# A two-block network on one core: an overflow branch moved behind the tenth of eleven expert passes, a first gather in halves, 8 KB weight runs and 512-column products

## The chip, the cores and the metric

One core of a Trainium2 chip runs the whole program, with batch 1 and 256 tokens. The metric is the device time of one execution in microseconds (us); the kernel before takes 1347.06 us, the median of three runs.

## The reference

The network has two blocks of two layers each, on 256 tokens with D = 1024, in float32. The change touches the feed-forward networks of the first block and the mixtures of experts of the second:

```python
def conv_glu_ffn(n, w_up, conv_w, conv_b, w_down):          # D_FF = 2816
    gate, up = jnp.split(n @ w_up, 2, axis=-1)
    gp = jnp.pad(gate, ((0, 0), (CONV_WIDTH - 1, 0), (0, 0)))
    conv = conv_b
    for j in range(CONV_WIDTH):
        conv = conv + gp[:, j:j + s] * conv_w[j]
    return (jax.nn.silu(conv) * up) @ w_down

def hier_moe(h, w_group, b_group, w_expert, b_expert, w_gate, w_up, w_down):
    ...            # the best of 4 groups by softmax, the best 2 of its 8 experts
    for g in range(N_GROUPS):
        a = jnp.einsum('nd,edf->nef', t, w_gate[g])
        b = jnp.einsum('nd,edf->nef', t, w_up[g])
        hid = jax.nn.silu(a) * b * combine[:, g, :, None]
        y = y + jnp.einsum('nef,efd->nd', hid, w_down[g])

def hybrid_layer(x, ...):
    ...            # three mixers side by side, w_in before and w_out behind them
    x = x + jnp.einsum('bsm,md->bsd', mixed, w_out)
    x = x + hier_moe(rms_norm_2(x, norm2_g), ...)
```

## The kernel before

In the order of time the program is: a hybrid mixer, FFN 0, a differential mixer, FFN 1 (block 1), then mixer2(0), moe(0), mixer2(1), moe(1) and the final norm (block 2). Layers of block 2 are written l=0 and l=1.

**Products in float32.** TensorE (PE) takes operands of a rounded type at full rate, so a dense product is made of three: each operand is split into a high part (ACT copies it into the rounded type) and a low part (DVE subtracts that from the value), and `mm3` (L273 to L278) adds high x high, high x low and low x high into one PSUM accumulator. For weights the parts are called whi (L241) and wlo (L242).

**The FFN** (L656 to L725) goes over D_FF in 11 groups of 256 gate and 256 up columns. `up(g)` loads and splits the weights, and makes two accumulators of 128 x 2 x 256, pa for the gate and pb for up, tokens along the columns: for each of two halves f of the group's columns, for each of the two and each of 8 k-slices, one `mm3` with 256 columns. Then DVE multiplies the gate by the rows' norm (gt, L692), ACT and DVE make the convolution (L696, L699), ACT the silu (L701), POOL a product (L702), DVE the product with pb (L703), and hh and hl (L260, L261) are the parts of the result. `down(g)` makes 24 matmuls of 512 columns into four accumulators; PE does `up(g + 1)` before `down(g)`, and at the end `down(10)` comes straight behind `down(9)`.

**The experts.** Per layer 32 experts go through in 11 passes of 3 (the last has 2). A pass has 128 slots in four quarters of 32: one for each expert and one more for the fullest expert of the three, whose number PE loads into a register (`load_most`, TENSOR_LOAD of most). Each pass has three pieces of weights, each of 3 MB (2 MB in the last pass): the first half of gate and up over k, the second half, and down. 33 pieces go through six places of SBUF in turn. SP issues them, one after the other, in the order of the program; a piece is issued when PE has read the last of the piece that lay in its place. Gate and up pieces have runs of 4 KB in memory; a down piece is loaded by two DMAs in runs of 4 KB (L1291).

Before pass 0, `moe` makes the router's logits, the norm (`stats`), the parts nh and nl of the tokens (L1047, L1041) and from the logits each token's experts and slots: a row of small DVE instructions from lg (L1051) over mask (L1065) to the one-hot matrix oh (L1252). `gather` (L1256) multiplies tokens by oh on PE, 32 matmuls for two passes (L1266), and ACT and DVE take the columns out by turns (xg, L1268 and L1269). `expert_pass` (L1299) then does: the slots' weights (L1311 to L1320, ohT, cq, cw), 32 matmuls of gate and up with 512 columns (L1328; the profile counts each twice), hid (L1335, L1336), its transposes (L1239), 16 matmuls of down (L1347), the parts yh and yl (L260, L261), and the scatter back to tokens (L1355), which the schedule puts between the next pass's halves.

**The overflow branch.** If a token does not fit its expert's slots, a slow loop computes it; `most_tokens` reads the largest overflow, and each engine branches on it. In these inputs the loop is not taken. The branch stands behind pass 3 (j == 3), with the pieces up to 17 issued ahead of it. On SP, the skipped block (L1169) still waits for every DMA lane and counts it up, one event for each of eight lanes; other engines whose later instructions wait for a lane in the new count wait for that event.

**Between the layers.** When moe(0) frees places, SP loads the weights of mixer2(1) into them (L230; the first two loads, of 416 columns, are split by ACT and DVE in pieces of 128 x 832), and later the first six pieces of l=1.

Of the kernel before, what the change touches and what calls it, by code (L numbers as in the profile page):

```python
# [119 lines left out]
class Net:  # L120
# [196 lines left out]
    def prep_T(self, pool, g, bufs=2):  # L317

        nc = self.nc
        hi, lo = self.big(pool, bufs)  # L320
# [335 lines left out]
    def ffn(self, l):  # L656
# [4 lines left out]
        with self.pool("ffn", 2) as pl:  # L661
# [3 lines left out]
            nT = self.prep_T(pl, self.g("ffn_norm", l))  # L665
# [11 lines left out]
            def up(g):  # L677
# [13 lines left out]
                gt = pl.tile([P, 2, S], F32, name="gt")  # L691
                nc.vector.tensor_tensor(gt, pg, rB, OP.mult)  # L692
# [10 lines left out]
                nc.vector.tensor_tensor(c, c, pu, OP.mult)  # L703
# [25 lines left out]
    def mixer2(self, l):  # L729
        nc, a = self.nc, self.a  # L730
        w = a["w_in_2"][l]
        with self.pool("hring2", 2) as self.hp, self.pool("mixT") as pt, \
# [143 lines left out]
            self.pooling(pl, pw, u, gp, oT)  # L876
            self.out_proj(oT, None, 1)
# [121 lines left out]
    def load_router(self, l):  # L999
# [11 lines left out]
        nc.vector.tensor_tensor(wr, wr, self.g("norm2_g_2", l)[:, :, None].to_broadcast([P, KD, 36]), OP.mult)  # L1011
        self.router = wr, br, gp

    def moe(self, l):
        nc, tc, a = self.nc, self.tc, self.a
        with self.pool("xb", XB, side="right") as xb, self.pool("moeh") as ph, \
# [17 lines left out]
            rs = self.stats()  # L1034
# [4 lines left out]
            def low(k0):  # L1039
                for tt in range(NT):  # L1040
                    nc.vector.tensor_tensor(nl[:, tt, k0:k0 + 4], hv(tt, k0), nh[:, tt, k0:k0 + 4].bitcast(F32), OP.subtract)  # L1041

            hv = lambda tt, k0: self.h[:, tt, :].rearrange("p (q k) -> p k q", k=KD)[:, k0:k0 + 4]
            with tc.issue_after(self.exp.ins):
                for k0 in (0, 4):
                    for tt in range(NT):
                        nc.scalar.activation(nh[:, tt, k0:k0 + 4], hv(tt, k0), AF.Copy)  # L1047
            low(0)
# [16 lines left out]
            nc.vector.tensor_tensor(mask.rearrange("p t (r e) -> p t r e", r=4), both, grid(ohg), OP.mult)  # L1065
# [41 lines left out]
            most = list(load_most(0, 1))  # L1107
# [312 lines left out]
```

## Time and profile before

| | us |
|---|---|
| median of 3 runs (lowest to highest) | 1347.06 (1345.64 to 1348.57) |
| the profiled execution | 1346.1 |
| its span, first to last instruction | 1344.2 |
| PE busy | 1213.9 (90% of the span) |
| DVE, ACT busy | 681.8, 555.1 |
| DMA, mean over the span | 249 GB/s, 335.21 MB |
| mean granted TensorE clock | 0.964 |

The stages lie, in us from the span's start, at about: FFN 0 136 to 331, FFN 1 444 to 646, moe(0) up to 989, moe(1) 1087 to 1335. Busy shares are means over stages with different limits, so the stages are read one by one, from the slices, the windows and the timeline. A timeline row has its start and length in us, the engine, the line and the operation with its tiles, and in brackets how long the engine was idle before it and what ended that. A row with xN stands for N instructions in succession. "SPq" is SP's queue of DMA issues, "PEq", "PEldq" are PE's sequencer.

### The profile page before, as it was taken

To read this page: it belongs to the slowest core of one execution; us is meant where nothing else is said; L and a number is where in the kernel's file an instruction comes from. 1 tells how busy PE (TensorE), PEld (TensorE's weight loads), DVE (VectorE), ACT (ScalarE), POOL (GpSimd) and SP (SyncE) were. 2 spreads that over 40 slices of the span, in tenths; PEclk is the share of its full clock that TensorE was granted. 3 is DMA by queue.
4 is the path that set the end of the run, shared out by engine and by line. 5 is a ranking of instruction groups with operands and counts; after the bars stand their busy time and mean duration, and the time that the engine had idled before them with its cause. 6 is when DMAs were issued, how large, how long until landed. Compare 5 with 4: busy or idle time off the path is not lost. (4 is left out here: it accounts for less than half of the span.)

```text
span 1344.2 us, 19870 instructions
## 1 busy us (share of the span) xinstructions
PE 1213.9 (90%) x7896; PEld 873.1 (65%) x7896; DVE 681.8 (51%) x1492; ACT 555.1 (41%) x994; POOL 72.9 (5%) x71
## 2 busy tenths in 40 slices
PE   7999999999999899999999798777899979949776
PEld 6867899998777799999877443233367663314332
DVE  6754755556888666556775622111166572202113
ACT  5664644444656444444675311111156632101112
POOL 0001001111000011111000000000000000000000
PEclk9999999999999999999999799889899989979988
DMA  7732455555545665551754399999996339999993
GB/s 266 251 132 93 142 184 188 188 172 177 188 142 160 228 224 184 180 181 53 287 221 175 130 408 409 360 407 409 409 386 270 142 140 358 408 363 399 409 409 142
DMA packets 144819, 335.21 MB, mean 249 GB/s; under 512 B 10448, under 2 KB 76627, under 8 KB 144723
## 3 DMA queue, kind: packets, MB, share of 16 engines
q1 hardware_dynamic: 143462, 332.94, 67.0%
q8 instruction: 65, 1.06, 0.3%
q10 hardware_dynamic: 1260, 0.95, 0.2%
q14 instruction: 32, 0.25, 0.1%
HBM read 332.82 MB, written 1.05 MB: 248 GB/s over the span
## 5 line engine op out<-in xcount | busy, mean ns | idle before, releaser
L241 ACT ACTIVATE whi<-x 128x2048 fp32r<-128x2048 f32 (+5 forms) x170 | 238.2, 1413 | 213.2 <-PE pa L277 106.0
L242 DVE TENSOR_TENSOR wlo<-x,whi 128x2048 fp32r<-128x2048 f32 (+5 forms) x166 | 277.1, 1678 | 95.8 <-ACT whi L241 88.4
L1328 PE MATMUL pa<-x,xg 128*32 128x512 f32 (+1 forms) x1408 | 179.9, 630 | 50.1 <-DVE yl L261 25.3
L276 PE MATMUL acc<-whi,big 128*128 128x512 f32 (+2 forms) x400 | 157.2, 396 | 2.6 <-ACT big L263 2.6
L277 PE MATMUL acc<-wlo,big 128*128 128x512 f32 (+2 forms) x400 | 156.0, 390 | 0.3 <-DVE wlo L242 0.3
L278 PE MATMUL acc<-whi,big 128*128 128x512 f32 (+2 forms) x400 | 154.1, 389 | 0.0
L1328 PEld LDWEIGHTS pa<-x,xg 128*32 128x32 f32 x1408 | 46.6, 115 | 151.7 <-issue 117.1
L1336 DVE SCALAR_TENSOR_TENSOR hid<-hid,cw,pa 128x128 f32<-128x128 f32 x44 | 15.1, 343 | 179.3 <-ACT hid L1335 179.3
L276 PE MATMUL pa<-big,whi 128*128 128x256 f32 x352 | 100.3, 285 | 3.7 <-DVE big L264 3.7
L276 PE MATMUL pb<-big,whi 128*128 128x256 f32 x352 | 99.8, 284 | 0.9 <-DVE rB L932 0.9
L278 PE MATMUL pa<-big,wlo 128*128 128x256 f32 x352 | 100.2, 285 | 0.0
L277 PE MATMUL pa<-big,whi 128*128 128x256 f32 x352 | 100.2, 285 | 0.0
L277 PE MATMUL pb<-big,whi 128*128 128x256 f32 x352 | 99.6, 283 | 0.0
L278 PE MATMUL pb<-big,wlo 128*128 128x256 f32 x352 | 99.6, 283 | 0.0
L1335 ACT ACTIVATE hid<-pa,cw 128x128 f32<-128x128 f32 x44 | 16.2, 367 | 195.0 <-PE pa L1328 185.8
L1347 PE MATMUL pa<-x,hidT 128*32 (+1 forms) x704 | 88.3, 620 | 5.4 <-DMA x<-in_w_down_dram 3.4
L276 PEld LDWEIGHTS acc<-whi,big 128*128 128x128 f32 x400 | 76.3, 191 | 18.6 <-ACT big L263 4.3
L278 PEld LDWEIGHTS acc<-whi,big 128*128 128x128 f32 x400 | 76.0, 190 | 15.8 <-issue 3.3
L277 PEld LDWEIGHTS acc<-wlo,big 128*128 128x128 f32 x400 | 76.4, 191 | 14.3 <-issue 1.7
L261 DVE TENSOR_TENSOR yl<-pa,yh 128x512 fp32r<-128x512 f32 x44 | 30.3, 691 | 108.4 <-ACT yh L260 108.4
L260 ACT ACTIVATE yh<-pa 128x512 fp32r<-128x512 f32 x44 | 26.2, 597 | 121.2 <-PE pa L1347 80.3
L276 PEld LDWEIGHTS pa<-big,whi 128*128 128x128 f32 x352 | 68.1, 193 | 4.9 <-issue 4.1
(350 smaller groups left out, 2201.2 us busy)
## 6 DMA issues: line engine op xcount, KB each, us to landing
x<-in_w_gate_dram SPq DMA_DIRECT2D x40, 1536.0 KB, 15.5
x<-in_w_up_dram SPq DMA_DIRECT2D x40, 1536.0 KB, 20.7
x<-in_w_down_dram SPq DMA_DIRECT2D x40, 1536.0 KB, 21.4
x<-in_ffn_w_up_dram SPq DMA_DIRECT2D x44, 1024.0 KB, 5.1
x<-in_ffn_w_down_dram SPq DMA_DIRECT2D x22, 1024.0 KB, 4.8
x<-in_w_in_dram SPq DMA_DIRECT2D x8, 1024.0 KB, 11.0
x<-in_w_out_dram SPq DMA_DIRECT2D x8, 1024.0 KB, 8.8
x<-in_hyb_w_in_dram SPq DMA_DIRECT2D x14, 512.0 KB, 6.1
```

The source lines that it names most:

```text
L241: self.hi = nc.scalar.activation(dst(hi), of(w), AF.Copy)
L242: self.lo = (eng or nc.vector).tensor_tensor(dst(lo), of(w), dst(hi).bitcast(F32), OP.subtract)
L260: self.hi = nc.scalar.activation(hi, psum, AF.Copy)
L261: self.lo = nc.vector.tensor_tensor(lo, psum, hi.bitcast(F32), OP.subtract)
L276: nc.tensor.matmul(out, ah, bh, start=start, stop=False)
L277: nc.tensor.matmul(out, ah, bl, start=False, stop=False)
L278: nc.tensor.matmul(out, al, bh, start=False, stop=stop)
L1328: nc.tensor.matmul(gu[s], xg[:, k, c0 + s.start:c0 + s.stop], x, start=k == 0, stop=k == KD - 1)
L1335: self.silu = nc.scalar.activation(hid, gu[:, 0, fs], AF.Silu, scale=cw[:, 1:2])
L1336: nc.vector.scalar_tensor_tensor(hid, hid, cw[:, 0:1], gu[:, 1, fs], op0=OP.mult, op1=OP.mult)
L1347: nc.tensor.matmul(pd[s], hT[f][:, s], x[:, hf * 512:hf * 512 + 512], start=f == 0, stop=f == 1)
```

## The change

It has seven parts.

1. In the FFN the normed tokens' high and low parts lie side by side in one tile nT, so that whi times both is one matmul with 512 columns, and wlo times the high part one with 256: two instead of three. The accumulator of one half f then has the two sums side by side; ACT copies the second out and DVE adds the first to it, into gt for the gate and into a new tile up.
2. In `moe` the parts of the tokens are made in another order: one part nh before the norm's chain, the low parts one behind the first nh, one behind the mask, two behind the first oh.
3. The first gather is in two halves of four k-slices. ACT alone takes out the first half; pass 0's first four k-slices are multiplied before the second half is gathered, and the slots' weights of pass 0 come after six. The register load for pass 0 stands behind the gather's first half.
4. The branch, with its loop, stands behind pass 9 (j == NP - 2), and all 33 pieces are issued before it.
5. Down pieces are read as "(p k)" and not as "(k p)": a partition takes two neighbouring rows of w_down, one run of 8 KB, in one DMA. The hidden units are taken with a step of 2 to fit.
6. The products of the router's weights with the norm's gains (wr) stand behind the pooling in mixer2(0), and behind pass 6 for l=1.
7. The scatter of pass 9 and the gather of pass 10 follow from 4.

The core of the diff:

```diff
@@ ffn, up(g)
-                pg = self.ps.tile([P, 2, S], F32, name="pa")
-                pu = self.ps.tile([P, 2, S], F32, name="pb")
+                gt = pl.tile([P, 2, S], F32, name="gt")
+                up = pl.tile([P, 2, S], F32, name="up")
                 for f in range(2):
+                    pg = self.ps.tile([P, 2, S], F32, name="pa")
+                    pu = self.ps.tile([P, 2, S], F32, name="pb")
...
-                                self.mm3(ps[:, f, :], (wh[:, k, fc], wl[:, k, fc]), (nT[0][:, k, :], nT[1][:, k, :]),
-                                         start=k == 0, stop=k == KD - 1)
-                nc.vector.tensor_tensor(gt, pg, rB, OP.mult)
+                                if k:
+                                    nc.tensor.matmul(ps[:, 0, :], wl[:, k, fc], nT[:, k, 0, :], start=False, stop=False)
+                                nc.tensor.matmul(ps, wh[:, k, fc], nT[:, k], start=k == 0, stop=k == KD - 1)
...
+                    for dst, ps in ((gt, pg), (up, pu)):
+                        nc.scalar.activation(dst[:, f, :], ps[:, 1, :], AF.Copy)
+                        nc.vector.tensor_tensor(dst[:, f, :], dst[:, f, :], ps[:, 0, :], OP.add)
+                nc.vector.tensor_tensor(gt, gt, rB, OP.mult)
@@ moe
+            high(0, 0)
+            rs = self.rstd(ss, D, EPS, "rs")
+            with tc.issue_after(self.exp.ins):
+                high(1, 0)
...
+            low(0, 0)
...
+            with tc.issue_after(self.last.ins):
+                low(1, 0)
...
+                    xg, rows = self.gather(pl, oh, nh, nl, gp)
+                    if j:
+                        rows(0, KD)
+                    else:
+                        rows(0, 4, False)
+                        with tc.issue_after(self.gathered.ins):
+                            most = list(load_most(0, 1))
+                between, more = lambda: None, lambda: None
+                if j == 0:
+                    between, more = lambda: rows(4, KD), lambda: most.extend(load_most(1, NP - 1))
...
-                if j == 3:
-                    self.prefetch(l, 0, 3 * (j + 1) + XH + XA + XB)
+                if j == NP - 2:
+                    self.prefetch(l, 0, 3 * NP)
                     with tc.If(self.most_tokens(pl, u) > 0):
@@ piece
-                src = a["w_down_2"][l].rearrange("g e (k p) n -> p (g e) k n", p=P)
-                for i in range(2):
-                    nc.sync.dma_start(v[:, :, i], src[:, e, i])
+                src = a["w_down_2"][l].rearrange("g e (p k) n -> p (g e) (k n)", k=2)
+                nc.sync.dma_start(t.rearrange("p (e m) -> p e m", e=m), src[:, e])
@@ expert_pass
         for k in range(KD):
+            if k == 4:
+                between()
...
-            fs = slice(f * P, f * P + P)
+            x = gu.rearrange("p a (m r) -> p a r m", r=2)[:, :, f]
```

The order of the instructions moves in three places. The first is PE at the start of pass 0 in l=1. "Row xN" is one instruction N times; L1266 is the gather and L1328 the products of the first half. Before, the second gather half stands among the first products:

```order
L1266 MATMUL pb<-oh,nh 128x256
L1104 TENSOR_LOAD most
L1104 ISA x2
...
L1328 ISA
L1328 MATMUL pa<-x,xg 32x512
L1266 MATMUL pb<-oh,nh 128x256 x2
L1266 MATMUL pb<-oh,nl 128x256 x2
...
L1328 MATMUL pa<-x,xg 32x512 x3
```

Now (the gather is L1295, the products L1370, the slots' weights L1345):

```order
L1295 MATMUL pb<-oh,nh 128x256 x3
...
L1295 MATMUL pb<-oh,nl 128x256 x2
L1120 TENSOR_LOAD most
L1120 ISA x2
L1370 ISA
L1370 MATMUL pa<-x,xg 32x512 x4
...
L1295 MATMUL pb<-oh,nh 128x256 x2
...
L1345 MATMUL pb<-idc,oh 128x218 x2
```

Of the 32 products of pass 0, the 16 that read piece 0 now all stand ahead of the second half of the gather.

The second is PE at the end of the stage, in l=1: L1347 is down, L1355 the scatter, L1311 the slots' weights. Before, the gather of pass 10 stands around pass 9's down products:

```order
L1266 MATMUL pb<-oh,nh 128x128 x2
L1347 ISA
L1347 MATMUL pa<-x,hidT 32x512 x4
...
L1266 MATMUL pb<-oh,nl 128x128 x2
L1311 MATMUL pb<-idc,oh 128x218 x2
L1328 MATMUL pa<-x,xg 32x512 x16
L1355 MATMUL acc<-yh,ohT 128x512
```

Now (down L1389, scatter L1397, slots' weights L1345; the rows of the loop that is skipped are left out):

```order
L1389 MATMUL pa<-x,hidT 32x512 x4
L1397 MATMUL acc<-yh,ohT 128x512
...
L1217 TENSOR_LOAD mi
L1196 COMPARE_AND_BRANCH
...
L1196 UNCONDITIONAL_BRANCH
L1295 MATMUL pb<-oh,nh 128x128 x2
...
L1345 MATMUL pb<-idc,oh 128x218 x2
L1370 MATMUL pa<-x,xg 32x512 x32
```

Down and scatter of pass 9 and the branch now all stand ahead of the gather of pass 10, and its products are in one row.

The third is ACT at the end of l=0, where whi 128x832 belongs to mixer2(1). Before:

```order
L1313 ACTIVATE ohT<-pb 128x256
L1335 ACTIVATE hid<-pa,cw 128x128 x2
L177 ACT_TABLE_LOAD
L260 ACTIVATE yh<-pa 128x512
L241 ACTIVATE whi<-x 128x832
```

Now:

```order
L1196 UNCONDITIONAL_BRANCH
L1302 ACTIVATE xg<-pb,gp 128x128 x4
L241 ACTIVATE whi<-x 128x832
L1347 ACTIVATE ohT<-pb 128x256
L241 ACTIVATE whi<-x 128x832
L1377 ACTIVATE hid<-pa,cw 128x128 x2
L177 ACT_TABLE_LOAD
L260 ACTIVATE yh<-pa 128x512 x2
```

The first two whi went from behind pass 10's hid to ahead of it.

## Rows read from the trace of the kernel before

**Rows 1.** The page, 40 slices of 33.6 us: DMA busy in tenths, GB/s.
```profile
DMA  7732455555545665551754399999996339999993
GB/s 266 251 132 93 142 184 188 188 172 177 188 142 160 228 224 184 180 181 53 287 221 175 130 408 409 360 407 409 409 386 270 142 140 358 408 363 399 409 409 142
```

**Rows 2.** Timeline of PE in FFN 0: start us, us, engine, line, operation.
```profile
234.17 0.28 PE L278 MATMUL pb<-big,wlo 128*128 128x256 f32 x1
234.29 0.39 PE L276 MATMUL acc<-whi,hh 128*128 128x512 f32 x1
234.52 0.40 PE L277 MATMUL acc<-wlo,hh 128*128 128x512 f32 x1
```

**Rows 3.** Timeline of layer 1's expert stage, its start: DVE, PE, SP.
```profile
1091.33 2.10 DVE L1041 TENSOR_TENSOR nl<-h,nh 128x512 fp32r<-128x512 f32 x2 [0.26 <-ACT nh L1047]
...
1099.61 0.55 PE L1266 MATMUL pb<-oh,nh 128*128 128x256 f32 x1 [1.93 <-DVE most L1101]
...
1103.83 1.05 PE L1328 MATMUL pa<-x,xg 128*32 x2
...
1111.13 0.37 SPq L1285 DMA_DIRECT2D x<-in_w_gate_dram  x1
...
1114.57 0.37 SPq L1285 DMA_DIRECT2D x<-in_w_gate_dram  x1
```

**Rows 4.** Windows: us, busy by engine (instructions), PEclk, DMA share, GB/s.
```profile
860.00:880.00 20.00, 18.61 (x144) 8.46 (x136) 6.01 (x17) 4.70 (x10) 0.00 (x0) 0.97 0.85 326
880.00:900.00 20.00, 13.56 (x108) 5.11 (x100) 4.25 (x17) 2.59 (x6) 0.31 (x1) 0.97 1.03 409
...
1200.00:1220.00 20.00, 10.62 (x73) 3.60 (x73) 3.20 (x11) 2.10 (x5) 0.00 (x0) 0.68 0.83 315
```

**Rows 5.** The branch's line L1169 (min/median/max ns, first to last start), and timeline.
```profile
L1169 SPq EVENT_SEMAPHORE  x16: 17/17/17, 848.3 to 1207.9; - x16
...
L1169 PEldq EVENT_SEMAPHORE  x2: 51/51/51, 827.4 to 1169.9; - x2
...
1163.98 3.64 PE L1347 MATMUL pa<-x,hidT 128*32 x32
...
1170.17 0.47 PE L1266 MATMUL pb<-oh,nh 128*128 128x256 f32 x2 [0.32 <-PEq L1169]
...
1208.00 1.08 ACT L260 ACTIVATE yh<-pa 128x512 fp32r<-128x512 f32 x2 [22.70 <-SPq L1169]
```

**Rows 6.** Timeline of layer 0's end: pass 9's second half, pass 10, mixer weights.
```profile
954.09 3.64 PE L1328 MATMUL pa<-x,xg 128*32 x32 [2.33 <-DMA x<-in_w_up_dram]
...
963.05 5.65 PE L1347 MATMUL pa<-x,hidT 128*32 x32
...
970.99 0.38 ACT L1313 ACTIVATE ohT<-pb 128x256 fp32r<-128x256 f32 x1 [0.17 <-PE pb L1311]
...
979.75 0.37 ACT L1335 ACTIVATE hid<-pa,cw 128x128 f32<-128x128 f32 x1 [8.38 <-PE pa L1328]
...
981.27 1.04 PE L1347 MATMUL pa<-x,hidT 128*32 128x512 f32 x2 [0.38 <-DVE hidT L1241]
...
985.07 0.89 ACT L241 ACTIVATE whi<-x 128x832 fp32r<-128x832 f32 x1
...
989.92 1.02 DVE L242 TENSOR_TENSOR wlo<-x,whi 128x832 fp32r<-128x832 f32 x1
```

**Rows 7.** Timeline of FFN 0's last group: DVE's gt and hl, PE's down.
```profile
317.21 0.69 DVE L692 TENSOR_TENSOR gt<-pa,rB 128x512 f32<-128x512 f32 x1 [3.79 <-PE pa L278]
...
324.86 0.69 DVE L261 TENSOR_TENSOR hl<-c,hh 128x512 fp32r<-128x512 f32 x1 [0.70 <-ACT hh L260]
...
325.98 0.40 PE L278 MATMUL acc<-whi,hl 128*128 128x512 f32 x1
```

**Rows 8.** Windows, columns as in rows 4, where mixer weights load.
```profile
980.00:985.00 5.00, 4.41 (x30) 1.21 (x31) 1.18 (x4) 2.20 (x4) 0.00 (x0) 1.00 1.09 351
```

**Rows 9.** The page's DMA issues: KB each, median us from issue to landing.
```profile
x<-in_ffn_w_up_dram SPq DMA_DIRECT2D x44, 1024.0 KB, 5.1
```

More of the change, by code (lines that the diff above doesn't have):

```diff
@@ L664, in ffn @@
             nc.scalar.dma_start(cw[3 * NF:4 * NF], a["ffn_conv_b"][l].rearrange("(f p) -> f p", p=P))
-            nT = self.prep_T(pl, self.g("ffn_norm", l))
+            nT = pl.tile([P, KD, 2, S], F32R, name="nT", bufs=1)
+            self.prep_T(pl, self.g("ffn_norm", l), parts=[nT[:, :, i, :] for i in range(2)])
             nT_split = self.hi, self.lo
@@ L1064, in moe @@
             mask = pl.tile([P, NT, NE], BF, name="mask")
-            nc.vector.tensor_tensor(mask.rearrange("p t (r e) -> p t r e", r=4), both, grid(ohg), OP.mult)
+            self.last = nc.vector.tensor_tensor(mask.rearrange("p t (r e) -> p t r e", r=4), both, grid(ohg), OP.mult)
+            with tc.issue_after(self.last.ins):
+                low(1, 0)
             pk = self.ps.tile([P, 3, NE], F32, name="pb")
@@ L1105, in load_most @@
                     mosti[:, j0:j1], engines=[mybir.EngineType.PE], min_val=0, max_val=2)[1]
-            most = list(load_most(0, 1))
             oh = self.one_hots(pl, s4, 0)
             with tc.issue_after(self.last.ins):
-                low(4)
+                for tt in range(NT):
+                    low(tt, 4)
             eg = pl.tile([P, NT, 4], F32, name="eg")
@@ L1223, in overflow @@
                 nc.vector.scalar_tensor_tensor(hid, hid, ce[:, tt:tt + 1], gu[tt][:, 1, :], op0=OP.mult, op1=OP.mult)
-                hT.append([self.hid_T(pl, hid[:, f * P:f * P + P]) for f in range(2)])
+                hT.append([self.hid_T(pl, hid[:, f:256:2]) for f in range(2)])
             for hf in range(2):
@@ L1260, in gather, with rows @@
         xg = pl.tile([P, KD, m * P], F32, name="xg", tag="xg", bufs=2)
[L1261 to L1270 removed]
+        def rows(k0, k1, both=True):
+            for k0 in range(k0, k1, 2):
+                pg = self.ps.tile([P, 2, m * P], F32, name="pb")
+                for k in range(2):
+                    for j, x in enumerate((nh, nl)):
+                        for tt in range(NT):
+                            self.gathered = nc.tensor.matmul(pg[:, k, :], x[:, tt, k0 + k, :], oh[:, tt],
+                                                             start=tt == 0 and j == 0, stop=tt == 1 and j == 1)
+                for k in range(2):
+                    d, i, s = xg[:, k0 + k, :], pg[:, k, :], gp[:, k0 + k:k0 + k + 1]
+                    if k and both:
+                        nc.vector.tensor_scalar(d, i, s, None, op0=OP.mult)
+                    else:
+                        nc.scalar.activation(d, i, AF.Copy, scale=s)
+        return xg, rows
     def piece(self, l, n):
@@ L1297, in prefetch, with expert_pass @@
             self.piece(l, n)
-    def expert_pass(self, pl, l, j, oh, xg, idc, py, most, scatter, more):
+    def expert_pass(self, pl, l, j, oh, xg, idc, py, most, scatter, between, more):
         nc = self.nc
@@ L1323, in expert_pass @@
         for k in range(KD):
+            if k == 4:
+                between()
+            if k == 6 and j == 0:
+                ohT, cw = weights()
             for c in range(4):
```

83 lines of the change are left out of this document (40 added, 43 removed).

## The prediction

> **What bounds the kernel now.** I read the slices of the page first, to see which resource each stage is short of. From slice 24 on, DMA is at 9 tenths and near 409 GB/s for most of both expert stages, with a dip in each [rows 1]. So the experts wait for weights, and the two dense FFNs, where DMA is about half busy, wait for TensorE: the timeline there shows matmuls of 256 columns starting 0.12 us apart and those of 512 columns 0.23 us apart, without gaps [rows 2].
>
> For the experts I then looked for what starts the stream and what breaks it. Pieces 0 to 5 lie in the six places before the stage begins. Piece 6 is issued when PE has done the first half of pass 0 (1111.13 us in l=1), piece 7 at 1114.57 [rows 3]. From there to the last landing DMA has one gap: in windows of 20 us it moves 409 GB/s, but 326 in 860 to 880 us (l=0) and 315 in 1200 to 1220 us (l=1) [rows 4]. The rows of the branch show why: SP's skipped block, from 848.3 on in l=0 and up to 1207.9 in l=1, waits for all eight DMA lanes before SP issues anything else. PE is long through the same branch by then, its last event there being at 1169.9, and gathers on at 1170.17. What does wait is ACT's yh, 22.70 us, since that instruction waits for lanes which only SP's skipped block releases [rows 5].
>
> Behind the last pieces comes a chain of compute. In l=0 pass 9's second half starts at 954.09, released by its weights, and pass 10's down product at 981.27: 27.2 us [rows 6], in which PE, and no longer DMA, sets the pace.
>
> **The change part by part.** The profiled execution took 1346.1 us (span 1344.2, 1.9 around it); the median of the runs is 0.96 above it.
>
> 1. *512-column up products.* A triple was three matmuls of 256 columns, 3 x 120 = 360 ns; it becomes one of 512 and one of 256, 234.5 + 120 = 354.5 ns [rows 2]. Two FFNs x 11 groups x 32 triples = 704, times 5.5 ns: **-3.9 us**. The Trainium skill, page TensorE: Matmul & The Clock Gate, section Back-to-back issue gap, gives a gap of N/2.4 + 2.5 ns for the isolated matmul at full clock; by that one matmul fewer saves 2.5 ns per triple, an estimate of 1.8 us in all. The rows show 120 ns where that rule has 109, so the sum goes by the rows. New in each group are four ACT copies and four DVE adds out of PSUM. In the steady groups they cost nothing: DVE idles 3.79 us before gt alone [rows 7]. At each FFN's end that cover is gone: hl ends at 325.55, and the first matmul that reads it stands at 325.98 [rows 7], 0.43 later. A copy and an add come ahead of gt (about 0.48 each, by gt's 0.69 for twice the columns), 0.96 less 0.43, and another add stands in DVE's row: **+0.7** per FFN, between 0.5 and 1.0. At its head the first group has two more accumulators to empty amid the splitting of weights, which no row shows: between 0.3 and 1.5, **+0.9** per FFN, the middle. Together -3.9 + 3.2 = **-0.7**, between -3 and +3.
>
> 2. *Gather in halves, low parts spread.* One of two nl halves (2.10 us for both [rows 3]) leaves the way to the logits, and one comes back behind the mask, beside PE's counting: the gather starts some 0.4 us earlier, at 1099.2. Then PE does 16 gather matmuls (4.2 us from 1099.61 to 1103.83, with a register load in them), loads the expert numbers, and does the first half of pass 0 at once (3.64, as its 32 records took at 954.09 [rows 6]); before, the second 16 stood between. 1099.2 + 3.7 + 0.7 + 3.64 = 1107.3 against 1111.13: piece 6 goes **3.8 us** earlier in each layer. Bounds: 2.5, if half of those products run at half speed, and 4.7, if the register load is hidden. Piece 7 follows by 6 us, within the 7.7 us that piece 6 takes at 409 GB/s.
>
> 3. *The branch behind pass 9.* All 33 pieces are issued ahead of it, so SP's wait breaks no stream any more. The gap was (409 - 326)/409 x 20 = 4.06 us in l=0 and (409 - 315)/409 x 20 = 4.60 in l=1 [rows 4]: **-8.7 us**.
>
> 4. *8 KB runs.* The mixer's weights, in runs of 1 to 4 KB, go at 351 GB/s in the window after the experts of l=0 [rows 8], experts in runs of 4 KB at 409 [rows 4]. A fixed time per run that fits these gives about 421 at 8 KB; 7 down pieces (22 MB) lie in each bound stretch, 53.8 us at 409 and 52.3 at 421. Between 0 and 1.5 I take **-1.0 per layer**. The Trainium skill, page DMA: Bandwidth & Descriptors, section Why small descriptors are slow, puts the cost on 256-byte packets and on 32 bytes of descriptor data per operation; by that an 8 KB run would save some 0.2 us per layer, an estimate that raises the sum by 1.6.
>
> 5. *The chain behind the last pieces.* Its order is now: pass 9's down product, its scatter, the branch, the whole gather of pass 10, its products. Before, the gather lay partly in the wait for pass 9's down weights. Counted from the start of pass 9's second half: its down weights are there 7.7 later (one piece at 409 GB/s); the product takes 5.65, as it did there [rows 6], to 13.4; from a down product's end to the gather behind the branch it was 1170.17 - (1163.98 + 3.64) = 2.6 [rows 5], to 16.0; 32 gather matmuls at 0.12 and the one-hot product 0.4, to 20.3; two halves of 3.64 and from hid to the down product 1.5 [rows 6], to 29.0. Before it was 27.2: **+1.8 per layer**. Piece 32 is there at 23, ahead of the yh that waits for SP, so the barrier itself costs nothing in l=1.
>
> 6. *Layer 0's ACT order.* SP now issues mixer2(1)'s weights only behind the barrier, at about 23.3 of the same count. On ACT the first whi stands ahead of pass 10's ohT and hid, on DVE wlo ahead of the pass's weights. A load of 0.85 MB takes about 4.6 us (1 MB: 5.1 [rows 9]), so ACT goes on at 27.9. whi 0.89, ohT 0.38, whi 0.89, beside them wlo 1.02 twice and small sums [rows 6] put DVE's first hid product at 31.4 instead of 27.9: **+3.6**. One wlo (1.02 at 989.92) no longer delays mixer2's first products: **-0.9**. The router's scaling goes behind the pooling, where DVE's work is not on the chain, and costs nothing.
>
> Sum: -0.7 - 7.6 - 8.7 - 2.0 + 3.6 + 2.7 = **-12.7 us**: 1333.4 for the profiled execution, **1334.4 for the median**.
>
> **The rivals.**
> *The branch holds every engine* (slower). If in its new place PE too came through only with SP, the gather of pass 10 would start at 24.5 instead of 16, on a PE that was idle: 0.21 us a matmul, as the 16 of rows 3 without their load, 6.9 instead of 3.9, and 1.3 more for the first products. That is 12.8 in l=1, and 12.8 less the 3.6 of step 6 in l=0: 22 more, 1356. It decides from 15.4 us lost on. For it: yh did wait 22.70 us. Against it: PE gathered in front of SP's last event in the kernel before [rows 5], and in the order now no row between branch and gather waits for a lane.
> *The early start is not had, and 8 KB runs go as 4 KB runs do*: +2.6 and +2.0, 1339. The second half is a change that does not do what it says.
> *The FFNs lose and layer 0's chain is later still*: 4 us in the FFNs, where PE would wait for accumulators in several groups, and 5 more until the first mixer weights: 1343. For it the longer DVE chains, against it the idle time in rows 7.
> *All covers hold*: FFN -3, no wait for w_in, 1.5 per layer from the runs: 1327.
>
> **How the numbers follow.** A measurement of this kernel tells about 0.2%, 2.7 us, from no change, so faster means below 1344.4. Forecast (1330 to 1338) 0.50, early start and runs absent 0.22, FFN and layer 0 losses 0.14 (0.09 of it within 0.2%), all covers hold 0.06, the branch 0.08. Faster 0.50 + 0.22 + 0.05 + 0.06 = 0.83, same 0.09, slower 0.08. The range, 1326 to 1345, leaves out the branch and the outer halves of its neighbours.
>
> **What would show it.** Right: no dip of DMA from piece 6 to the last landing; piece 6 some 3.8 us earlier after the logits; an FFN group in 16.95 instead of 17.12 us; PE's gather of pass 10 ahead of SP's last event; in l=0 an ACT that is idle before whi until a DMA. Wrong: PE idle between pass 9's scatter and that gather until SP's event, down pieces slower than 409 GB/s, or PE waiting within the FFN's groups for the copies.

## The result and the profile after

The changed kernel takes **1322.78 us**, the median of four runs (1322.38 to 1325.76), against 1346.35 (1345.36 to 1348.57) for the kernel before on the same chip: the ratio is 0.9828, with a 95% interval of 0.9808 to 0.9847. The forecast was 1334.4, so the gain is 23.6 us where 12.7 was expected. The sign and most of the mechanisms were right, the size was not: the result lies 3.2 us below the range of 1326 to 1345.

The profiled execution is the slowest of the four, 1325.76 us with a span of 1324.0; the span fell by 20.2, so 3.4 of the 23.6 us do not show in the profiles below. The page's slices, to be read against rows 1:

```profile
DMA  7732455555535765551664499999997248999993
GB/s 270 248 130 90 156 191 191 191 175 172 198 104 183 227 223 190 189 191 64 262 240 191 160 405 412 412 415 410 364 377 280 96 191 339 407 413 412 414 411 130
```

Neither expert stage has a dip any more, and but for its first full slice (405 and 407) each plateau lies at 410 to 415 GB/s, where most slices had 407 to 409. In the windows in which rows 4 showed the two gaps:

```profile
860.00:880.00 20.00, 16.03 (x111) 5.52 (x110) 3.75 (x14) 2.32 (x5) 0.00 (x0) 0.91 1.02 412
880.00:900.00 20.00, 12.72 (x108) 6.61 (x110) 2.63 (x7) 2.55 (x6) 0.00 (x0) 1.00 1.02 413
1200.00:1220.00 20.00, 16.82 (x126) 5.67 (x122) 3.92 (x17) 3.19 (x7) 0.00 (x0) 0.91 1.02 412
```

I then cut the program into pieces at the first residual sum of each stage (L388 on DVE) and, within the expert stages, at two more marks: the issue of piece 6 (the stage's weights begin to stream) and the start S of pass 9's second half (954.09 in rows 6). The last two columns are lengths before less after, in us, and what the prediction had for them:

| stretch | before | after | change | forecast |
|---|---|---|---|---|
| hybrid mixer | 132.13 | 131.62 | -0.5 | 0 |
| FFN 0 | 194.99 | 192.80 | -2.2 | -0.35 |
| differential mixer | 121.53 | 118.21 | **-3.3** | 0 |
| FFN 1 | 193.69 | 191.87 | -1.8 | -0.35 |
| mixer2(0) | 98.21 | 98.23 | 0.0 | 0 |
| l=0: to piece 6 | 27.99 | 21.84 | **-6.1** | -3.8 |
| l=0: piece 6 to S | 185.55 | 180.84 | -4.7 | -5.1 |
| l=0: S to the end | 33.44 | 41.10 | **+7.7** | +5.4 |
| mixer2(1) | 96.88 | 97.64 | +0.8 | -0.9 |
| l=1: to piece 6 | 26.72 | 22.03 | -4.7 | -3.8 |
| l=1: piece 6 to S | 185.95 | 182.10 | -3.9 | -5.6 |
| l=1: S to the end | 35.09 | 33.81 | **-1.3** | +1.8 |

The rest of the span, the final norm, is 0.1 shorter. Four places made the surprise: both FFNs (-3.3 beyond the forecast), a mixer that was not in the sum at all (-3.3), the heads of the expert stages (-3.2) and the end of layer 1 (-3.1). Layer 0's end gave 2.3 of it back, the streams from piece 6 to S 2.1 and mixer2(1) 1.7.

**The mixer.** The change moves the scaling of the router's weights, and the prediction priced that at nothing. Before, this is what it did, by the timelines of DVE, PE and POOL in the kernel before:

```profile
435.94 0.42 DVE L635 COPY o<-pb 128x256 f32<-128x256 f32 x1 [1.14 <-PE pb L634]
437.08 2.63 DVE L1011 TENSOR_TENSOR wr<-wr,gains 128x288 f32<-128x288 f32 x1 [0.72 <-DMA wr<-in_w_group_dram]
439.63 0.41 DVE L635 COPY o<-pb 128x256 f32<-128x256 f32 x1
...
443.51 0.68 PE L649 MATMUL pb<-ident,o 128*128 128x128 f32 x4 [2.31 <-DVE o L643]
...
L242 POOL TENSOR_TENSOR wlo<-x,whi x2: 2398/2410/2421, 434.6 to 437.0; 128x1024 fp32r<-128x1024 f32 x2
```

(The last row is by line: ns of the shortest, median and longest, first and last start.) In the changed kernel the two copies of o follow each other:

```profile
433.29 0.42 DVE L635 COPY o<-pb 128x256 f32<-128x256 f32 x1 [1.14 <-PE pb L634]
435.13 0.42 DVE L635 COPY o<-pb 128x256 f32<-128x256 f32 x1 [1.42 <-PE pb L634]
...
439.01 0.68 PE L649 MATMUL pb<-ident,o 128*128 128x128 f32 x4 [0.49 <-DVE o L643]
...
L1024 DVE TENSOR_TENSOR wr<-wr,gains x2: 450/450/450, 718.9 to 879.4; 128x288 f32<-128x288 f32 x2
```

The multiplication first waited 0.72 us for its weights and then took 2.63 us, though the same instruction takes 0.45 in both places of the changed kernel. It stood between the two copies from which the mixer's last norm is made, so these were 3.69 us apart instead of 1.84, and PE was idle 2.31 us before its transposes instead of 0.49. During the output product the granted clock was 0.67 before and is 1.00 now, by the windows of before and after:

```profile
445.00:450.00 5.00, 5.00 (x15) 4.05 (x16) 1.80 (x3) 0.00 (x0) 0.00 (x0) 0.67 1.07 366
...
440.00:445.00 5.00, 4.53 (x20) 3.76 (x21) 2.23 (x4) 0.42 (x1) 0.00 (x0) 1.00 1.06 370
```

The slow multiplication began just behind POOL's second wlo (437.0) and ended at 439.71, just behind that one's end (437.0 + 2.4). The Trainium skill, page SBUF — State Buffer, section Who interferes with whom, says that a DVE instruction with two SBUF inputs and a GpSimd one that reads SBUF hold one shared port pair by turns, the later one blocked until the earlier ends; the trace agrees, 2.63 us being the 2.3 that POOL still had and 0.3 more.

**The FFN's groups.** Rows 2 had three matmuls of 256 columns for a triple; now:

```profile
238.65 0.28 PE L694 MATMUL pa<-nT,wlo 128*128 128x256 f32 x1
238.77 0.40 PE L695 MATMUL pa<-nT,whi 128*128 128x512 f32 x1
239.00 0.28 PE L694 MATMUL pa<-nT,wlo 128*128 128x256 f32 x1
```

A pair is 0.35 us; from one POOL product of a group to the next it is 16.81 us on average instead of 17.12 in the seven steady intervals, so 0.31 a group where 32 x 5.5 ns = 0.18 were forecast.

**The head of an expert stage.** In l=1, to be read against rows 3:

```profile
1079.27 1.07 DVE L1054 TENSOR_TENSOR nl<-h,nh 128x512 fp32r<-128x512 f32 x1
...
1088.90 0.98 PE L1295 MATMUL pb<-oh,nh 128*128 128x256 f32 x3 [2.40 <-DVE most L1117]
...
1092.48 3.64 PE L1370 MATMUL pa<-x,xg 128*32 x32
...
1096.18 0.37 SPq L1319 DMA_DIRECT2D x<-in_w_gate_dram  x1
...
1102.40 0.37 SPq L1319 DMA_DIRECT2D x<-in_w_gate_dram  x1
```

Counted from the stage's start (1084.41 before, 1074.15 after) the gather begins 0.45 earlier, as forecast, but the products follow it after 3.58 us, with no gap for the register load.

**The branch and layer 0's end.** By its line, and the timelines of PE, ACT and DVE, against rows 5 and 6:

```profile
L1196 SPq EVENT_SEMAPHORE  x16: 17/17/17, 950.9 to 1301.3; - x16
...
L1196 PEldq EVENT_SEMAPHORE  x2: 51/51/51, 949.3 to 1292.6; - x2
...
949.52 0.41 PE L1295 MATMUL pb<-oh,nh 128*128 128x128 f32 x2 [0.36 <-PEq L1196]
...
953.81 7.07 PE L1370 MATMUL pa<-x,xg 128*32 128x512 f32 x64
967.18 0.47 PE L1266 MATMUL pb<-ident,hid 128*128 128x128 f32 x1 [6.30 <-DVE hid L1378]
968.04 1.91 PE L1389 MATMUL pa<-x,hidT 128*32 128x512 f32 x2 [0.38 <-DVE hidT L1268]
...
963.63 0.90 ACT L241 ACTIVATE whi<-x 128x832 fp32r<-128x832 f32 x1 [9.78 <-DMA x<-in_w_in_dram]
```

PE gathers pass 10 at 949.52 and 1292.93, ahead of SP's last event, so the rival in which the branch holds every engine is out. ACT sits 9.78 us before the next mixer's first whi and reaches it 28.2 us behind S (forecast: 27.9); hid waits behind it, and PE 6.30 us for hid. The product that follows then runs its first two matmuls in 1.91 us and the others in 4.87, instead of 1.04 and 3.63 in l=1: the granted clock is 0.60 in the window from 965 to 970 us.

```profile
965.00:970.00 5.00, 2.44 (x4) 0.48 (x4) 2.67 (x9) 2.60 (x4) 0.00 (x0) 0.60 1.09 350
```

### The profile page after: what moved, and what is told of

The parts are those of the page before. It is cut to its first block, busy times and chain, and to the rows that moved or that the text cites. A ratio compares the mean times of both kernels' runs of the same rounds, so it can differ in the third digit from the quotient of the medians.

```text
span 1324.0 us, 18576 instructions
## 1 busy us (share of the span) xinstructions
PE 1203.5 (91%) x7192; PEld 830.1 (63%) x7192; DVE 710.6 (54%) x1576; ACT 585.7 (44%) x1086; POOL 71.1 (5%) x71
## 5 line engine op out<-in xcount | busy, mean ns | idle before, releaser
L1370 PE MATMUL pa<-x,xg 128*32 128x512 f32 (+1 forms) x1408 | 175.9, 641 | 34.2 <-DMA x<-in_w_up_dram 32.4
L1370 PEld LDWEIGHTS pa<-x,xg 128*32 128x32 f32 x1408 | 47.0, 116 | 142.0 <-issue 130.6
L695 PE MATMUL pa<-nT,whi 128*128 128x512 f32 x352 | 129.8, 404 | 3.7 <-DVE nT L264 3.7
L695 PE MATMUL pb<-nT,whi 128*128 128x512 f32 x352 | 126.8, 397 | 0.9 <-DVE rB L944 0.9
L1378 DVE SCALAR_TENSOR_TENSOR hid<-hid,cw,pa 128x128 f32<-128x128 f32 x44 | 15.1, 343 | 192.8 <-ACT hid L1377 192.8
L1389 PE MATMUL pa<-x,hidT 128*32 (+1 forms) x704 | 90.7, 644 | 5.0 <-DMA x<-in_w_down_dram 3.7
L694 PE MATMUL pa<-nT,wlo 128*128 128x256 f32 x308 | 87.4, 284 | 0.0
L694 PE MATMUL pb<-nT,wlo 128*128 128x256 f32 x308 | 86.0, 279 | 0.0
L695 PEld LDWEIGHTS pa<-nT,whi 128*128 128x128 f32 x352 | 67.4, 192 | 17.9 <-issue 4.1
L695 PEld LDWEIGHTS pb<-nT,whi 128*128 128x128 f32 x352 | 65.8, 188 | 13.3 <-DVE rB L944 1.3
L276 PE MATMUL acc<-whi,hh 128*128 128x512 f32 x176 | 69.8, 397 | 0.0
L277 PE MATMUL acc<-wlo,hh 128*128 128x512 f32 x176 | 69.8, 396 | 0.0
```

The costliest lines, as they stand in the source:

```text
L276: nc.tensor.matmul(out, ah, bh, start=start, stop=False)
L277: nc.tensor.matmul(out, ah, bl, start=False, stop=False)
L694: nc.tensor.matmul(ps[:, 0, :], wl[:, k, fc], nT[:, k, 0, :], start=False, stop=False)
L695: nc.tensor.matmul(ps, wh[:, k, fc], nT[:, k], start=k == 0, stop=k == KD - 1)
L1370: nc.tensor.matmul(gu[s], xg[:, k, c0 + s.start:c0 + s.stop], x, start=k == 0, stop=k == KD - 1)
L1378: nc.vector.scalar_tensor_tensor(hid, hid, cw[:, 0:1], x[:, 1], op0=OP.mult, op1=OP.mult)
```

## The experiments

My theory after the table: the mixer's 3.3 us are the moved multiplication's, the FFNs give 4.0 by themselves, the early piece 6 arrives at the end, and the branch's move is nearly cancelled by the mixer's splits behind it in layer 0. The rivals: the prediction's own prices, and for each part that something else made the difference. The kernel before ran beside every kernel on its chip.

**1. The scaling alone.** The kernel before, with one edit:

```diff
-        nc.vector.tensor_tensor(wr, wr, self.g("norm2_g_2", l)[:, :, None].to_broadcast([P, KD, 36]), OP.mult)
         self.router = wr, br, gp
+        self.scale_router = lambda: nc.vector.tensor_tensor(wr, wr, ...)
@@ mixer2(0), behind the pooling, and pass 6 of moe(0)
+                with self.tc.issue_after(self.lo.ins):
+                    self.scale_router()
```

> The kernel before with the router's scaling (wr times gains) moved behind mixer2(0)'s pooling and behind pass 6, as in the change, and nothing else. Theory from the two traces: the instruction stood between the last two o copies of the differential mixer, waited 0.72 us for wr and took 2.63 us beside POOL's wlo, all of it on the way to the output projection: -3.3 us. Rival, as predicted: DVE's work there is hidden, 0 us.

Measured: 1343.24 us (1340.11 to 1345.12, six runs), ratio 0.9975 (0.9963 to 0.9988). The differential mixer took 118.1 instead of 121.5 us, the FFNs and mixer2(0) the same within 0.1. Its first residual sums of FFN 0 and of the mixer:

```profile
327.34 0.69 DVE L388 TENSOR_TENSOR h<-h,acc 128x512 f32<-128x512 f32 x1 [1.57 <-PE acc L278]
...
445.43 0.69 DVE L388 TENSOR_TENSOR h<-h,acc 128x512 f32<-128x512 f32 x1 [1.41 <-PE acc L278]
```

The multiplication in its old place was what the mixer lost its time to. (The profile is of the fastest of the six, 1340.11 us; it is 3.0 us shorter in layer 1's expert stage too, which the edit does not touch and the median does not show.)

**2. The FFN's part alone**, with the `prep_T` that it needs, in the kernel before.

```diff
-            nT = self.prep_T(pl, self.g("ffn_norm", l))
+            nT = pl.tile([P, KD, 2, S], F32R, name="nT", bufs=1)
+            self.prep_T(pl, self.g("ffn_norm", l), parts=[nT[:, :, i, :] for i in range(2)])
...
```

> The kernel before with the FFN of the change (512-column up products, the new evacuations) and nothing else. Theory from the traces: group interval 17.12 to 16.81 us, ten intervals per FFN, a head later by 0.6 and an end that costs nothing: -2.0 per FFN, -4.0 us. Rival, as predicted: the same products, but 0.7 at each end and 0.9 at each head lost, -0.7 us.

Measured: 1337.88 us (1333.30 to 1340.38, four runs), ratio 0.9922 (0.9898 to 0.9947). The profile has FFN 0 at 192.8 and FFN 1 at 191.9, that is 2.2 and 1.8 shorter, 4.0 together as the theory had it. The rest was not expected by either: the differential mixer also fell, to 118.2. The multiplication is still between the two copies, by DVE's and POOL's timelines:

```profile
434.28 0.56 DVE L1020 TENSOR_TENSOR wr<-wr,gains 128x288 f32<-128x288 f32 x1 [0.44 <-DMA wr<-in_w_group_dram]
...
432.10 4.99 POOL L242 TENSOR_TENSOR wlo<-x,whi 128x1024 fp32r<-128x1024 f32 x2 [110.92 <-ACT whi L241]
...
L242 POOL TENSOR_TENSOR wlo<-x,whi x2: 2432/2518/2605, 432.1 to 434.5; 128x1024 fp32r<-128x1024 f32 x2
```

but it now takes 0.56 us. It began 0.24 us before the first of POOL's two ended (432.10 + 2.43 = 434.53) and ended 0.31 behind that end, as it had ended 0.32 behind the second one's in the kernel before; POOL's second, which started while it ran, took 2.61 us instead of 2.40. So the loss was a collision, whose price hangs on how much of POOL's instruction is left when DVE's starts (2.3 us before, 0.24 here), and runs 1 and 2 each avoid the same 3.4 us; they must not be added. The mixer and the FFNs are 7.3 us of the 7.5 by which this profile is shorter; the medians differ by 9.2, and the four runs spread over 7.1.

**3. The branch back behind pass 3**, the rest as changed.

```diff
-                if j == NP - 2:
-                    self.prefetch(l, 0, 3 * NP)
+                if j == 3:
+                    self.prefetch(l, 0, 3 * (j + 1) + XH + XA + XB)
```

> The changed kernel with the branch and the issue ahead of it back behind pass 3, all else as changed. Theory: the gap in the DMA stream comes back (4.1 and 4.6 us), the chain behind the last pieces gets its old order (1.8 shorter per layer by the prediction, by the traces nothing in l=1) and layer 0's mixer weights come early again (about 7.7 shorter there): the two nearly cancel in l=0, so +1 to +4 us against the changed kernel. Rival: the branch's move is where most of the gain is, +9 us or more; a third: the move gives nothing or costs, 0 or below.

Measured: 1323.26 us (1321.65 to 1331.46, four runs), ratio 0.9834 (0.9797 to 0.9872): no difference from the changed kernel that this can tell. That rules out the rival of +9 us, but does not decide between the theory's +1 to +4 and the third, a move that gives nothing. The stream's gap is back where SP waits, in the windows

```profile
840.00:860.00 20.00, 6.70 (x44) 1.77 (x48) 2.31 (x8) 1.36 (x3) 0.00 (x0) 0.57 0.80 313
1180.00:1200.00 20.00, 14.95 (x114) 6.30 (x107) 5.15 (x15) 3.75 (x8) 0.00 (x0) 0.95 0.84 329
```

and piece 6 to S takes 185.3 and 183.9 us, 4.4 and 1.8 longer. But layer 0's stage is 4.5 shorter in all (239.3 against 243.8), and layer 1's 3.1 longer. So step 3's gap is real, and what the branch's new place costs behind S in layer 0 (41.1 us from S to the end, against 31.8 here) takes it away again.

**4. The next mixer's splits behind pass 10's SiLU**, the rest as changed. Only layer 0 has a next mixer.

```diff
-            self.ready = [self.split(v[:, k:k + 2]) for k in (0, 2)]
+            with nullcontext() if l == 0 else self.tc.issue_after(self.silu.ins):
+                self.ready = [self.split(v[:, k:k + 2]) for k in (0, 2)]
```

> The changed kernel with the first two splits of mixer2(1)'s weights ordered behind the last silu of pass 10 in layer 0, all else as changed. Theory: ACT's wait for the weights' DMA (9.78 us before whi) no longer stands ahead of pass 10's hid, PE is not idle 6.3 us before its transposes and keeps its full clock for the down product: -4 to -6 us against the changed kernel, from pass 9's second half to the residual 36 instead of 41.1. Rival: the splits are needed by mixer2(1) anyway and only move behind the chain, 0 to -1 us.

Measured: **1318.04 us** (1317.88 to 1318.19, four runs), ratio 0.9782 (0.9765 to 0.9798). Layer 0's stage takes 236.05 us, 7.7 less than in the profile of the changed kernel. ACT and PE at its end:

```profile
964.34 1.69 ACT L241 ACTIVATE whi<-x 128x832 fp32r<-128x832 f32 x2 [0.49 <-DMA x<-in_w_in_dram]
...
962.91 1.04 PE L1389 MATMUL pa<-x,hidT 128*32 128x512 f32 x2 [0.38 <-DVE hidT L1268]
963.89 0.33 PE L1266 MATMUL pb<-ident,hid 128*128 128x128 f32 x1
964.15 3.63 PE L1389 MATMUL pa<-x,hidT 128*32 128x512 f32 x30
```

PE waits 0.87 us for hid, as in l=1, and not 6.30, and the down product's 30 records take 3.63 us again. From S to the end it is 33.8 us instead of 41.1. The splits that stood ahead of hid had cost both the wait and the lowered clock that followed it.

**5. The changed kernel once more**, for the spread of its stages.

> The changed kernel itself, unaltered, beside the three others of this call. Both theories: 1322 to 1326 us, block by block within 0.5 us of the profile of the changed kernel, but for the end of layer 1's expert stage, whose length (237.9 us there) the run with the branch back behind pass 3 and the run with the splits behind the SiLU had at 241.1 and 237.6. It says how far one profile's stage lengths may be read.

Measured: 1324.50 us (1322.26 to 1325.02, four runs), ratio 0.9832 (0.9816 to 0.9848). Both FFNs are 0.6 shorter than in the first profile, layer 0's expert stage is 245.4 (243.8), layer 1's 236.1 (237.9). The expected 0.5 us a block was too narrow. So 2 us in one profile's expert stage say nothing, and the 1.3 us at layer 1's end in the table are no finding by themselves.

**6. Down pieces in 4 KB runs**, the rest as changed, the hidden units in halves again.

```diff
-                src = a["w_down_2"][l].rearrange("g e (p k) n -> p (g e) (k n)", k=2)
-                nc.sync.dma_start(t.rearrange("p (e m) -> p e m", e=m), src[:, e])
+                src = a["w_down_2"][l].rearrange("g e (k p) n -> p (g e) k n", p=P)
+                for i in range(2):
+                    nc.sync.dma_start(v[:, :, i], src[:, e, i])
...
```

> Down pieces in 4 KB runs again (and the hidden units in two halves instead of odd and even), the rest as in the changed kernel. Theory: the piece stream runs at 409 instead of about 412.5 GB/s, so some 181 us from piece 6 to the last product become 182.6, in each layer: 1.5 to 3.5 us slower in all. Rival: the runs' length changes nothing that the stream shows, and what shortened it was the branch alone: within 0.8 us.

Measured: 1326.79 us (1325.77 to 1330.30, four runs), ratio 0.9862 (0.9846 to 0.9879), 2.3 above run 5 beside it. The windows, against the changed kernel's above:

```profile
860.00:880.00 20.00, 15.49 (x108) 5.33 (x100) 3.71 (x13) 2.31 (x5) 0.00 (x0) 0.91 1.03 409
880.00:900.00 20.00, 13.46 (x98) 6.79 (x98) 2.29 (x7) 2.15 (x5) 0.00 (x0) 0.91 1.03 408
1200.00:1220.00 20.00, 15.15 (x112) 5.44 (x106) 3.88 (x17) 2.59 (x6) 0.00 (x0) 0.93 1.03 409
```

The rate is 408 to 410 in every window of both stages, at a DMA share of 1.02 to 1.03, so the run's length does change it. But three windows make the changed kernel look faster than it is: over the 18 windows of 20 us from 760 to 940 and 1100 to 1280 its two profiles (the first and run 5's) have means of 411.4 and 411.9 GB/s, and this run 408.8. If the down pieces are a third of the bytes, that is 417 to 418 for them, below the forecast's 421. The Trainium skill, page DMA: Bandwidth & Descriptors, section Why small descriptors are slow, would have 0.2 us a layer, an estimate. The 2.3 us between the medians are 1.1 a layer, near the forecast's 1.0, but the two intervals overlap (0.9846 to 0.9879 here, 0.9816 to 0.9848 in run 5), and the stretch from piece 6 to S, 180.8 and 182.2 us here, is the same as in the first profile of the changed kernel (180.8 and 182.1) and 1.1 longer in one layer than in the second (181.0 and 181.0). So what the long runs are worth in time, this run alone leaves open between nothing and 2.3 us.

**7. The head of the expert stage as before**, the rest as changed: the gather of pass 0 whole, the parts in their old order, the register load and the slots' weights early.

```diff
-                    if j:
-                        rows(0, KD)
-                    else:
-                        rows(0, 4, False)
-                        with tc.issue_after(self.gathered.ins):
-                            most = list(load_most(0, 1))
+                    rows(0, KD)
...
```

> The expert stage's head as it was (gather of pass 0 whole, low parts in their old order, register loads ahead of the one-hots, weights ahead of the product), the rest as in the changed kernel. Theory: piece 6 is issued some 6.2 us (layer 0) and 4.7 us (layer 1) later and the stream's end with it, nearly in full, since the DMA engines are busy at 0.93 or more from there to the last piece: 8 to 11 us slower. Rival: the earlier issue finds the queue still full of pieces 0 to 5, so less than half arrives at the end: 2 to 5 us slower.

Measured: 1334.17 us (1333.56 to 1334.71, four runs), ratio 0.9909 (0.9893 to 0.9926): 9.7 above run 5, the largest single part of the change. Piece 6 is issued 27.0 and 27.7 us into the stage, 4.6 and 5.6 later than in the mean of the changed kernel's two profiles, and the two stages are 248.7 and 241.6 us long, 4.1 and 4.5 more than those means. What a piece 6 is early arrives at the end nearly in full.

**8. Splits behind the SiLU, and the branch behind pass 3 in layer 0 alone.**

```diff
-                if j == NP - 2:
-                    self.prefetch(l, 0, 3 * NP)
+                if j == (3 if l == 0 else NP - 2):
+                    self.prefetch(l, 0, 3 * NP if l else 3 * (j + 1) + XH + XA + XB)
```

> The splits of the next mixer's first pieces ordered behind pass 10's SiLU, and in layer 0 the branch behind pass 3 again, in layer 1 behind pass 9. Theory: layer 0's 4.5 us that the branch behind pass 3 seemed to give came from the splits, which then found their piece landed; with the splits out of the way only the refill gap is left, so layer 0 is 2 to 4 us longer than with the splits moved alone (236.1 us), 1320 to 1322 us in all. Rival: layer 0 wants the early branch by itself, and both gains add up: 1313 to 1316 us.

Measured: 1323.79 us (1323.33 to 1326.50, four runs), ratio 0.9830 (0.9814 to 0.9847), 5.7 above run 4; the profile is of the slowest of the four. Both gains do not add up, so the rival is out; the theory's 2 to 4 us are exceeded too: piece 6 to S alone is 5.2 longer than in run 4 (185.6 against 180.4). Layer 0's stage is 243.8 us where run 3, with the same place for the branch, had 239.3. S is reached 207.5 us into the stage in both, but behind it PE's rows differ. Run 3, then this one:

```profile
940.37 4.93 PE L1370 MATMUL pa<-x,xg 128*32 x32 [4.02 <-DMA x<-in_w_up_dram]
...
949.52 3.64 PE L1389 MATMUL pa<-x,hidT 128*32 x32
...
955.33 3.64 PE L1370 MATMUL pa<-x,xg 128*32 128x512 f32 x32
```

```profile
940.00 6.34 PE L1370 MATMUL pa<-x,xg 128*32 x32 [4.01 <-DMA x<-in_w_up_dram]
...
951.69 5.62 PE L1389 MATMUL pa<-x,hidT 128*32 x32
...
959.49 3.64 PE L1370 MATMUL pa<-x,xg 128*32 128x512 f32 x32
```

The same 4.0 us of idle time precede both. The granted clock differs, by the windows of run 3 and of this one:

```profile
940.00:945.00 5.00, 4.63 (x32) 1.28 (x32) 0.00 (x0) 0.00 (x0) 0.00 (x0) 0.70 1.01 419
950.00:955.00 5.00, 4.95 (x47) 2.47 (x39) 1.64 (x3) 1.65 (x4) 0.00 (x0) 1.00 1.03 413
```

```profile
940.00:945.00 5.00, 5.00 (x24) 1.33 (x28) 0.00 (x0) 0.00 (x0) 0.00 (x0) 0.50 1.02 419
950.00:955.00 5.00, 5.00 (x25) 2.37 (x28) 0.70 (x2) 0.40 (x2) 0.00 (x0) 0.50 1.03 410
```

Between S and pass 10, 4.5 us are lost. PE had also waited 1.64 us for the weights of pass 9's first half here, and 0.20 in run 3. Whether that makes the difference was not settled; two runs of run 3's kernel lie 10 us apart (1321.65 and 1331.46).

**9. Run 4's kernel again, and with pass 10's gather moved into pass 9.** PE waits 2 to 5 us for the up piece in the middle of pass 9 while 3.9 us of gather stand behind the branch. The gather gets a place of its own, since the branch's loop uses xg's two.

```diff
+                if j == NP - 2:
+                    nxt = []
+                    def between():
+                        o = self.one_hots(pl, s4, NP - 1)
+                        x, rows = self.gather(pl, o, nh, nl, gp, "xl")
+                        rows(0, KD)
+                        nxt.extend((o, x))
+                if j == NP - 1:
+                    oh, xg = nxt
...
```

> The kernel with the next mixer's first splits behind pass 10's SiLU, once more, beside the one that follows. Theory: 1317 to 1319.5 us, expert stages of 236 and 237.6 us within 1.5. Rival: its first 1318.0 was one chip's luck: 1321 to 1324.

> The same, and pass 10's one-hots and gather (32 matmuls, 3.9 us behind the branch) put between the halves of pass 9's product, where PE waits 3.2 us (layer 0) and 2.3 us (layer 1) for the up piece. Theory: behind the last pieces PE alone sets the end, so 3.9 us less the 0.7 to 1.6 us by which the gather outlasts the wait, in each layer: 4.5 to 6.5 us faster than the splits alone, 1311.5 to 1313.5 us. Rival: the last pieces land no sooner, so pass 10's products wait for them in the gather's place: within 1 us of the splits alone.

Measured: run 4's kernel 1317.59 us (1314.82 to 1318.48, four runs), ratio 0.9774 (0.9741 to 0.9807), so its gain is found again on another chip; its stages are 238.0 and 237.1 us long, the first 0.4 over what was expected, since pass 9's down product took 6.47 us there instead of 3.64. With the gather moved **1313.22 us** (1312.30 to 1314.16, four runs), ratio 0.9748 (0.9716 to 0.9779). The timeline of PE in layer 0:

```profile
935.67 3.64 PE L1379 MATMUL pa<-x,xg 128*32 x32 [1.62 <-DMA x<-in_w_up_dram]
...
943.17 5.03 PE L1398 MATMUL pa<-x,hidT 128*32 x32 [1.60 <-DMA x<-in_w_down_dram]
...
950.73 0.45 PE L1354 MATMUL pb<-idc,oh 128*128 128x218 f32 x2 [0.30 <-PEq L1205]
951.11 7.07 PE L1379 MATMUL pa<-x,xg 128*32 128x512 f32 x64
```

The wait for the up piece is 1.62 us, where run 4's kernel had 3.23 and 4.02 in its two profiles, and behind the branch PE goes straight to the slots' weights and pass 10's product, 15.4 us behind S instead of 18.9 in run 4 (22.3 in its second profile). The stages are 235.0 and 234.4 us long. All four of its runs are faster than every run of the changed kernel and of run 4's; the gain over run 4's beside it, 4.4 us, is just under the 4.5 to 6.5 expected, and the two intervals overlap.

## Why the prediction was right or wrong

**Where it failed.** The mechanisms of the expert stages were right in the main. The result left the range because two terms were wrong by 3.3 us each: the router's scaling (step 6), put at nothing, and the FFN's sum (step 1), put at -0.7. The heads (step 2) were 3.2 us better than priced.

**Right.** The DMA gaps closed with the branch's move, PE passed the branch without SP, and ACT waited for the mixer's weights until 28.2 us behind S, where 27.9 was forecast. The run length raised the rate, though less than forecast.

**Step 6, "The router's scaling ... costs nothing": the largest blind spot.** I looked for what the moved multiplication would disturb in its new place and not at what it disturbed in its old one. It cost 3.4 us there (run 1), where DVE's wait for wr and the collision with POOL held up the mixer's last norm, and its row, 2.63 us against 0.45 for the second of its two instances, was in the trace of before. A moved instruction's old place has a price too.

**Step 1, "Together -3.9 + 3.2 = -0.7": mis-sized.** Counted on PE, from the last up product of one group to that of the next, the nine intervals behind the second group gave -2.5 and -2.6, since eight of them fell from 17.12 to 16.81 us. So the saving of a triple was mis-sized, 9.7 ns (0.31 us / 32) and not 5.5: eleven groups at 0.31 would be -3.4 in each FFN, where 1.9 was forecast. The two heads, to the last up product of the second group, are 0.2 shorter and 0.7 longer with two groups' saving in them, so they lost about 0.5 and 1.3 (forecast +0.9 each; in run 5's profile both are 0.6 shorter again). The ends, from the last up product to the first residual sum, were priced at +0.7 each and went from 7.06 to 7.52 and 7.09: +0.5 in FFN 0 and nothing in FFN 1. At FFN 0's end the longer chain of DVE was as forecast: hl is done at 323.12, and the down product that reads it stands at 323.18, on a PE that was late there. Run 2 puts the whole at -4.0. On the pair the Trainium skill, page TensorE: Matmul & The Clock Gate, section Back-to-back issue gap, would have saved 2.5 ns, by its formula for the isolated matmul; the 0.31 us a group are 9.7.

**Step 2, "piece 6 goes 3.8 us earlier": the upper bound came true.** 4.7 was named for a hidden register load, and layer 1 shows just that (-4.7): the products follow the gather at once. Layer 0 gave 6.1, more than the bound. A head scatters by up to 1.5 us from profile to profile; the means of the four profiles with the old head (27.7 and 27.1 us) and of the eight with the new one (22.0 and 22.6) differ by 5.8 and 4.6. What gives layer 0 the more was not taken apart. Run 7 confirms that this time arrives at the end.

**Steps 3 and 4 together** were priced at -10.7, and piece 6 to S shows -8.6. All profiles together split it. In layer 0 the stretch is 185.3 to 185.7 us with the branch behind pass 3 and 179.3 to 181.0 with it behind pass 9, with runs of either length: the branch gives 4.8 or 4.9 (forecast 4.06) and the runs 0.2 or 0.3 (forecast 1.0). In layer 1 the branch gives 3.9 with 4 KB runs and 2.6 with 8 KB (one profile each has the 4 KB runs with the new place and the 8 KB runs with the old), less than the 4.60 read from one window, and the runs between 0.8 and 2.2.

**Step 5, "+1.8 per layer".** For layer 0 S to pass 10's down product grew by 5.45, as 1.8 + 3.6 foresaw, but the split was not so: PE began pass 10's products 18.4 us behind S where 20.3 was forecast, and waited; ACT's wait for the weights alone set the time. For layer 1 it fell from 28.87 to 27.59, instead of rising to 29.0: the 27.2 of rows 6 were layer 0's and were taken for both, and pass 9's down product took 3.64 us, not 5.65 as in rows 6 or 5.71 as in layer 1 before. Neither the rise nor the fall is a finding, though: from S to the end layer 1 took 32.0 to 36.0 us in four profiles with the old order there, and 32.8 to 35.7 in seven with the new one.

**Step 6's other end.** What came on top in layer 0 was the clock: after 6.30 us of idle time PE did the next product in 1.91 + 4.87 us instead of 1.04 + 3.63, and the stretch behind it became 2.2 longer. And mixer2(1) was not 0.9 shorter but 0.8 longer; it is 97.4 to 97.7 in all profiles of the changed kernel's variants, with the branch in either place, and why stays open. Run 4 takes ACT's wait away, and with it the lowered clock.

**The rivals.** The branch that holds every engine fell by PE's rows (949.52, where SP's first event is at 950.9). "All covers hold" came nearest with 1327, but by its number alone: it had no wait for w_in, and ACT's 9.78 us are one. The range had no case in which a thing outside the sum was faster, only cases in which the listed terms were.

So of the 23.6 us, the FFNs and the mixer give 7.3 (the table, with runs 1 and 2), the head 9.7 by the medians and 8.6 by the stages (run 7), and the long runs some 1 to 2.5 (run 6 and the stretches to S). The branch's move, the first thing in the change's name, gives nothing that run 3 can tell as it was made, and 5.7 us in layer 0 once the splits are out of its way (run 4 against run 8). These sum to 17 to 19.5; the rest is not assigned to any part.

## What to carry to other kernels

When an instruction is moved, read its row in the old place first: a duration far above that of its twin is time that the move gives back. When a wait on a queue is moved to the end of a stream, look at which later stage's work already stands in the engines' order behind that queue, and put it behind the last thing that the stage needs (run 4); then fill the wait that is left with work that stood behind it (run 9). Stage lengths of a single profile of this kernel differ by up to 2 us, so an argument on less needs the medians of several runs.

## What was not expected of the hardware

A DVE product of 128x288 took 2.63 instead of 0.45 us, ending 0.3 us behind a POOL product that had started just before it. Reads in runs of 8 KB for a third of the bytes raised a stream from a mean of 408.8 to 411.4 and 411.9 GB/s at a DMA share of 1.01 to 1.03 in both. And idle times of PE of the same 4.0 us were followed once by a product of 4.93 us and once by one of 6.34 with the granted clock at 0.50 in two of the next three windows of 5 us, which moved a stage by 4.5 us.
